# Rotating images by 90 degrees: the first 4 MB in neighbouring partitions, stored quadrant by quadrant

## Chip, cores and metric

The kernel runs on one core of a Trainium2 chip. The metric is the device time of one execution in microseconds (us), the median of several runs. Profiles come from one execution that the hardware profiler recorded.

## What is computed

The input is a batch of 32 x 3 images of 256 x 256 float32 values, 25.17 MB. Each image is turned by a quarter clockwise:

```
np.rot90(x, k=-1, axes=(-2, -1))
```

Output row j of an image is column j of the input, read from the bottom up. No arithmetic is done; 25.17 MB come in and 25.17 MB go out.

## The kernel before

All images are taken as one stack of 24576 rows of 256 values. R = 16 rows are one unit of 16 KB, so an image is 16 units. A group of size s holds 128 x s units: s units of 16 KB in each of 128 SBUF partitions. `sizes` is (2, 2, 2, 4, 2): five groups of 4.19, 4.19, 4.19, 8.39 and 4.19 MB, each with a tile of its own (u0 to u4), so that the whole input lies in SBUF and no buffer is used twice, apart from the small ones named below.

**Loads (lines 50 to 59).** A group is split into halves a = 0, 1 and into I = s interleaved sets i. One transfer fills the partitions i, i + I, i + 2I and so on, for both halves: 64 partitions x 2 rows of 16 KB for a group of size 2, and 32 partitions x 2 rows of 32 KB for the group of size 4, each 2 MB. The first and the last transfer are cut in two of 1 MB (lines 56 and 57), so there are 14 loads. All are issued by SP in the order of the program; the last but one is called `mark`.

**Turning (`turn_group`, lines 61 to 79).** VectorE's transpose turns blocks of 32 x 32 inside each block of 32 partitions (a quadrant). For a group of size 2 there are four such instructions, for the four quarters (low or high rows and columns of a unit), each 128 x 2048 elements; for the group of size 4 there are eight. They work in place. So the first quarter (line 69) is written to a spare tile in PSUM or to the tile `extra`, the other three (line 74) into the group's tile, and ScalarE then copies the first quarter to its place (line 79). The order in which elements are written, `c r k i`, is chosen so that after the transposes a partition holds whole output rows, of the images that its number stands for. VectorE takes the groups in order, and each waits for its loads.

**Stores (lines 81 to 87).** A group goes out by two transfers, even partitions and odd partitions: 64 partitions x s rows of 16 KB. The stores are issued by SP after all loads, and the first one waits for `mark`, so that loads and stores do not mix in the queue. Later stores stand behind it in the queue of SP. Each transfer uses one of eight semaphores in turn; a transfer that takes one again waits until its earlier user has landed.

Of the kernel before, what the change touches and what calls it, by code (L numbers as in the profile page):

```python
# [1 line left out]

# [4 lines left out]


@with_exitstack  # L10
def kernel(
    ctx: ExitStack,
    tc: tile.TileContext,
    x: bass.AP,
    out: bass.AP,
):

    nc = tc.nc
    fp32 = mybir.dt.float32

    B, C, H, W = x.shape
    P = nc.NUM_PARTITIONS
    R = 16
    E = R * W  # L30
    hw = R // 2
    low, high = slice(0, hw), slice(hw, R)

    rows_in = x.rearrange("b c h w -> (b c h) w")
    rows_out = out.rearrange("b c h w -> (b c h) w")

    sizes = (2, 2, 2, 4, 2)
    first = [sum(sizes[:n]) for n in range(len(sizes))]
    groups = [
        ctx.enter_context(tc.tile_pool(name=f"group{n}", bufs=1)).tile([P, s, E], fp32, name=f"u{n}")  # L40
        for n, s in enumerate(sizes)
    ]
    psum = ctx.enter_context(tc.tile_pool(name="psum", bufs=1, space=bass.MemoryType.PSUM))
    spare = [psum.tile([P, E // 2], fp32, name=f"spare{h}") for h in range(2)]
    extra = ctx.enter_context(tc.tile_pool(name="extra", bufs=1)).tile([P, E // 2], fp32, name="extra")

    def rows_of(rows, n):
        return rows[first[n] * P * R : (first[n] + sizes[n]) * P * R]

    for n in range(len(sizes)):  # L50
        I = sizes[n]
        ld = rows_of(rows_in, n).rearrange("(a i m r) w -> i m a (r w)", a=2, i=I, m=P // I)
        to = groups[n].rearrange("p s f -> p (s f)").rearrange("p (a f) -> p a f", a=2)
        for i in range(I):
            if (n, i) in ((0, 0), (len(sizes) - 1, I - 1)):
                mark = nc.sync.dma_start(out=to[i::I, 0], in_=ld[i][:, 0])  # L56
                nc.sync.dma_start(out=to[i::I, 1], in_=ld[i][:, 1])  # L57
            else:
                nc.sync.dma_start(out=to[i::I], in_=ld[i])

    def turn_group(n, held):
        I = sizes[n]
        T = I // 2
        K = W // (R * T)
        u = groups[n].rearrange("p s f -> p (s f)")
        src = u.rearrange("p (a t r g c) -> p t c r g a", a=2, t=T, r=R, c=R)
        dst = u.rearrange("p (i c k t r) -> p t c r k i", i=I, c=R, k=K, t=T)[:, ::-1, :, ::-1, ::-1, :]
        for t in range(T):
            nc.vector.transpose(  # L69
                out=held[t].rearrange("p (i c k r) -> p c r k i", i=I, c=hw, k=K)[:, :, ::-1, ::-1, :],  # L70
                in_=src[:, t, low, low])
        for c, r in ((low, high), (high, high), (high, low)):
            for t in range(T):
                nc.vector.transpose(out=dst[:, t, c, r], in_=src[:, t, c, r])  # L74
        back = u.rearrange("p (i c k t r) -> p t i c k r", i=I, c=R, k=K, t=T)[:, ::-1]
        for t in range(T):
            kept = held[t].rearrange("p (i c k r) -> p i c k r", i=I, c=hw, k=K)
            for i in range(I):
                nc.scalar.copy(out=back[:, t, i, low, :, high], in_=kept[:, i])  # L79

    for n, held in enumerate(([spare[0]], [extra], [spare[1]], spare, [extra])):
        turn_group(n, held)

    for n in range(len(sizes)):
        st = rows_of(rows_out, n).rearrange("(a i m r) w -> a m i (r w)", a=2, i=sizes[n], m=P // 2)
        for a in range(2):
            put = nc.sync.dma_start(out=st[a], in_=groups[n][a::2])
            if (n, a) == (0, 0):
                tc.add_manual_dep(put.ins, mark.ins.name, mybir.DependencyInfo(
                    mybir.DependencyClass.Sync, mybir.DependencyReason.SCHED_ONLY), reason="stores after loads")  # L90


# [1 line left out]
_INS = ['x']  # L94
_OUTS = [((32, 3, 256, 256), 'float32')]


# [23 lines left out]
```

## Time and profile before

| what | value |
|---|---|
| median of 3 runs | 123.49 us (123.46 to 123.56) |
| the profiled execution | 123.59 us |
| its span (first to last recorded event) | 121.8 us |
| VectorE busy | 86.9 us, 24 transposes |
| ScalarE busy | 13.2 us, 16 copies and a table load |
| moved by DMA | 50.33 MB, 413 GB/s over the span |
| issues on SP | 24 transfers: 14 loads, 10 stores |

Busy times are those of one engine's instructions added up. The slices cut the span in 40 equal parts, of 3.05 us each here; a digit is the busy share in tenths, and the line of GB/s is what the 16 DMA engines moved. "SPq" is SP's queue of transfers: its instruction issues a transfer and goes on, and the transfer lands later.

### The profile page before, as it was taken

How to read it: one execution, taken by the hardware profiler on the slowest of the kernel's cores; microseconds unless marked ns; L12 is line 12 of the kernel's file. 1: busy time of each engine (PE TensorE's matmuls, PEld its weight loads, DVE VectorE, ACT ScalarE, POOL GpSimd, SP SyncE). 2: the span in 40 equal slices, each digit the busy share in tenths (PEclk: the TensorE clock that was granted, in tenths of full speed). 3: DMA queues.
4: the chain of work that ended last, by engine and by line, in shares of the span. 5: the costliest groups of instructions: out<-in, count | busy, mean ns of one | idle time of the engine just before them, and what ended most of it. 6: DMA issues, size and time to landing. Idle time of an engine off the chain costs nothing.

```text
span 121.8 us, 131 instructions
## 1 busy us (share of the span) xinstructions
DVE 86.9 (71%) x24; ACT 13.2 (11%) x17; POOL 0.2 (0%) x4
## 2 busy tenths in 40 slices
DVE  0000599999999999999999999999999991000000
ACT  0000400006000060001400000003720006000000
POOL 0000000000000000000000000000000000000000
DMA  4999999999999999999999999999999999999994
GB/s 86 387 430 430 430 430 436 430 430 430 479 420 441 420 452 409 398 430 430 425 430 409 430 425 430 430 430 430 430 425 420 425 430 430 430 430 425 430 430 178
DMA packets 3200, 50.33 MB, mean 413 GB/s; under 512 B 384, under 2 KB 384, under 8 KB 384
## 3 DMA queue, kind: packets, MB, share of 16 engines
q1 hardware_dynamic: 3200, 50.33, 97.5%
HBM read 25.17 MB, written 25.17 MB: 413 GB/s over the span
## 4 chain that ended last, share of the span: by engine, by line
DVE 60%; issue 12%; DMA 9%; SPq 1%; ACT 1%; ACTq 1%; DVEq 0%
DVE u L74 42%; DVE spare L69 12%; DMA u<-in_x_dram 9%; DVE extra L69 6%; ACT u L79 1%; ACTq L116 1%; SPq L56 0%; SPq L57 0%; DVEq L69 0%
## 5 line engine op out<-in xcount | busy, mean ns | idle before, releaser
L74 DVE STREAM_TRANSPOSE u<-u 128x2048 f32<-128x2048 f32 x18 | 65.4, 3650 | 0.5
L69 DVE STREAM_TRANSPOSE spare<-u 128x2048 f32<-128x2048 f32 x4 | 14.2, 3581 | 13.5 <-DMA u<-in_x_dram 13.5
L79 ACT COPY u<-spare 128x512 f32<-128x512 f32 (+1 forms) x12 | 8.0, 743 | 51.7 <-DVE u L74 51.7
L69 DVE STREAM_TRANSPOSE extra<-u 128x2048 f32<-128x2048 f32 x2 | 7.7, 3862 | 0.0
L79 ACT COPY u<-extra 128x1024 f32<-128x1024 f32 x4 | 4.0, 1043 | 24.6 <-DVE u L74 24.6
L79 ACT ACT_TABLE_LOAD x1 | 1.3, 1283 | 13.5 <-DMA u<-in_x_dram 13.5
L105 POOL MEMSET const-bfloat16-1.0<- 128x1 bf16 x1 | 0.1, 101 | 0.0
L105 POOL MEMSET const-uint8-127<- 128x1 uint8 x1 | 0.1, 101 | 0.0
L105 POOL MEMSET const-float32-0.0<- 128x1 f32 x1 | 0.1, 98 | 0.2 <-issue 0.2
L105 POOL MEMSET const-float32-1.0<- 128x1 f32 x1 | 0.1, 98 | 0.0
## 6 DMA issues: line engine op xcount, KB each, us to landing
u<-in_x_dram SPq DMA_DIRECT2D x10, 2048.0 KB, 30.4
out_dram<-u SPq DMA_DIRECT2D x8, 2048.0 KB, 16.4
out_dram<-u SPq DMA_DIRECT2D x2, 4096.0 KB, 16.7
u<-in_x_dram SPq DMA_DIRECT2D x4, 1024.0 KB, 20.6
```

The lines of the kernel that those rows point to most:

```text
L69: nc.vector.transpose(out=held[t].rearrange("p (i c k r) -> p c r k i", i=I, c=hw, k=K)[:, :, ::-1, ::-1, :], in_=src[:, t, low, low])
L74: nc.vector.transpose(out=dst[:, t, c, r], in_=src[:, t, c, r])
L79: nc.scalar.copy(out=back[:, t, i, low, :, high], in_=kept[:, i])
L105: nc = _bacc.Bacc("TRN2", target_bir_lowering=False, num_devices=1)
L116: with _tile.TileContext(nc) as tc:
```

## The change

Group 0, the first 4.19 MB, is laid out differently; the other groups are not touched. It is loaded by two transfers, one per half a: unit p of the half goes to partition p, so neighbouring units lie in neighbouring partitions (128 partitions x one row of 16 KB, 2 MB each). Since an image is 16 units, a quadrant then holds two whole images of each half. In `turn_group` the elements of group 0 are written in the order `c r i k` in place of `c r k i`; the counts and sizes of the instructions are the same. The stores of group 0 go by quadrant q and half a: 16 partitions (every second one of 32) x 2 rows of 16 KB, 0.5 MB each, eight in place of two. The first load of the kernel is no longer cut in two, so there are 13 loads and 16 stores.

```diff
-    for n in range(len(sizes)):
+    ld = rows_of(rows_in, 0).rearrange("(a p r) w -> a p (r w)", a=2, p=P)
+    for a in range(2):
+        nc.sync.dma_start(out=groups[0][:, a], in_=ld[a])
+    for n in range(1, len(sizes)):
...
-            if (n, i) in ((0, 0), (len(sizes) - 1, I - 1)):
+            if (n, i) == (len(sizes) - 1, I - 1):
...
-        dst = u.rearrange("p (i c k t r) -> p t c r k i", i=I, c=R, k=K, t=T)[:, ::-1, :, ::-1, ::-1, :]
+        def to(tile, c, t):
+            if n == 0:
+                return tile.rearrange("p (i c k t r) -> p t c r i k", i=I, c=c, k=K, t=t)[:, ::-1, :, ::-1, :, ::-1]
+            return tile.rearrange("p (i c k t r) -> p t c r k i", i=I, c=c, k=K, t=t)[:, ::-1, :, ::-1, ::-1, :]
+        dst = to(u, R, T)
         for t in range(T):
-            nc.vector.transpose(
-                out=held[t].rearrange("p (i c k r) -> p c r k i", i=I, c=hw, k=K)[:, :, ::-1, ::-1, :],
-                in_=src[:, t, low, low])
+            nc.vector.transpose(out=to(held[t], hw, 1)[:, 0], in_=src[:, t, low, low])
...
-    for n in range(len(sizes)):
+    st = rows_of(rows_out, 0).rearrange("(a q i g r) w -> q a g i (r w)", a=2, q=4, i=2, r=R)
+    for q in range(4):
+        for a in range(2):
+            put = nc.sync.dma_start(out=st[q, a], in_=groups[0][q * P // 4 + a : (q + 1) * P // 4 : 2])
+            if (q, a) == (0, 0):
+                tc.add_manual_dep(put.ins, mark.ins.name, mybir.DependencyInfo(
+                    mybir.DependencyClass.Sync, mybir.DependencyReason.SCHED_ONLY), reason="stores after loads")
+    for n in range(1, len(sizes)):
         st = rows_of(rows_out, n).rearrange("(a i m r) w -> a m i (r w)", a=2, i=sizes[n], m=P // 2)
         for a in range(2):
-            put = nc.sync.dma_start(out=st[a], in_=groups[n][a::2])
...
+            nc.sync.dma_start(out=st[a], in_=groups[n][a::2])
```

More of the change, by code (lines that the diff above doesn't have):

```diff
@@ L82 @@
         turn_group(n, held)
-    for n in range(len(sizes)):
+    st = rows_of(rows_out, 0).rearrange("(a q i g r) w -> q a g i (r w)", a=2, q=4, i=2, r=R)
[6 more added lines that the diff above has]
+    for n in range(1, len(sizes)):
         st = rows_of(rows_out, n).rearrange("(a i m r) w -> a m i (r w)", a=2, i=sizes[n], m=P // 2)
         for a in range(2):
[L87 to L90, printed above, removed]
+            nc.sync.dma_start(out=st[a], in_=groups[n][a::2])
 _INS = ['x']
```

## The prediction, made before the changed kernel ran

> **What bounds the kernel now.** I read the busy shares and the slices of the page first, then the queue, then a table of windows cut where one group's transfers end and the next begin, then what SP waited for. On the page:
>
> ```profile
> DVE 86.9 (71%) x24; ACT 13.2 (11%) x17; POOL 0.2 (0%) x4
> ...
> DMA  4999999999999999999999999999999999999994
> GB/s 86 387 430 430 430 430 436 430 430 430 479 420 441 420 452 409 398 430 430 425 430 409 430 425 430 430 430 430 430 425 420 425 430 430 430 430 425 430 430 178
> ...
> q1 hardware_dynamic: 3200, 50.33, 97.5%
> ```
>
> The reader is to see that the 16 DMA engines are busy in every slice but the first and last, at 420 to 440 GB/s: 50.33 MB at 430 GB/s are 117.0 us of a span of 121.8. VectorE is busy for 71% only, ScalarE for 11%. The time is the time of the queue, as long as something always stands in it. The chain of waits names VectorE for 60%, because each transpose follows another without a gap; but the table of windows (columns: length, VectorE, ScalarE, GpSimd busy and count, TensorE clock, DMA share, GB/s) shows no fall of the rate:
>
> ```profile
> 2.00:13.40 11.40, 0.00 (x0) 0.00 (x0) 0.00 (x0) 1.00 1.01 402
> 13.40:33.00 19.60, 19.36 (x6) 3.21 (x3) 0.00 (x0) 1.00 1.02 435
> 33.00:52.40 19.40, 19.26 (x6) 1.99 (x2) 0.00 (x0) 1.00 1.00 429
> 52.40:62.20 9.80, 9.77 (x4) 1.93 (x2) 0.00 (x0) 1.00 1.01 430
> 62.20:71.90 9.70, 9.63 (x4) 0.00 (x0) 0.00 (x0) 1.00 0.99 421
> 71.90:91.50 19.60, 19.53 (x6) 4.11 (x8) 0.00 (x0) 1.00 1.01 427
> 91.50:111.20 19.70, 9.40 (x3) 1.99 (x2) 0.00 (x0) 1.00 1.01 429
> 111.20:121.80 10.60, 0.00 (x0) 0.00 (x0) 0.00 (x0) 1.00 0.84 357
> ```
>
> From 2.0 to 62.2 us the 25.17 MB come in, from 62.2 to 121.0 they go out. The rows are, in order: group 0 in; groups 1 and 2 in; group 3 in; group 4 in; group 0 out (4.19 MB in some 9.75 us); groups 1 and 2 out; group 3 out; group 4 out. Two rows matter below. Group 3 comes in by transfers that touch 32 partitions each, every fourth one, at 429 GB/s. Group 0 goes out by transfers that touch 64 partitions each, every second one, at 421 GB/s. Every transfer of the kernel before is spread over all 128 partitions in this manner. One more view, the DMA queue's own waits:
>
> ```profile
> SPq L87 <- DMA u<-in_x_dram: 31.1, 1, 31.1
> SPq L87 <- DVE u L74: 29.7, 2, 19.2
> ```
>
> The stores of group 0 are held only until the marked load has landed (31.1 us at one wait); groups 3 and 4 are held for VectorE (and briefly ScalarE), issued at 89.2 and 103.0 us, while the queue still has earlier stores: group 2 until 91.5, group 3 until 111.2. So VectorE has about 1 us of cover at group 3 (a first packet starts about 1.4 us after its issue: first issue at 0.73, first bytes at 2.1) and about 7 us at group 4.
>
> **The change, part by part.**
>
> *The loads of group 0.* Three transfers (1, 1 and 2 MB, 64 partitions) become two of 2 MB over 128 neighbouring partitions. Bytes and 16 KB rows are the same 256. One issue goes: L56 took 0.60 us and L57 0.57 us for 64 rows, L59 0.62 for 128; the first issue stays at about 0.6, so the first bytes still come at 2.1 us, and later issues lie beside running transfers. The stretch from 2.0 to 13.4 runs at 402 GB/s and not at 430; the missing 28/430 of 11.4 us are 0.74 us, and that bounds any gain: between 0 and -0.7 us. A loss is bounded by one issue, +0.6. I take 0: the slow part is the first packet of each engine, and the new load has such a packet too. Group 0's transposes need both transfers, that is all 4 MB, as before.
>
> *VectorE.* The four transposes of group 0 keep 2048 elements per partition; only the order of the written elements changes (inner run of 16 at a step of 64 B, outer 2, where it was inner 2 over 16). No row shows that order. The nearest rows: inner 2 takes 3.62 us, inner 4 (group 3) 3.55 to 3.70, the slowest of all (into the extra tile) 3.87. So I bound it by ±0.3 us each, ±1.2 us for four, take 0, and it is covered by 1 us at group 3 and by more if stores of group 0 take longer. Without cover the excess over 1 us, 0.2 us, would be seen. VectorE, ScalarE and their counts of instructions are otherwise unchanged.
>
> *Issue and waits of the stores.* Two stores become eight: six more issues on SP of at most 0.65 us (the first of L87 took 0.67, 128 rows; the new one has 32 rows), 3.9 us in all. They begin at 59.85 us while the last load still has 2.3 us to run; each carries 0.52 MB, 1.22 us of transfer at 430 GB/s, so SP is ahead of the queue by 1.22 - 0.65 us each time: nothing on the path. If issues took the 1.37 us that the slowest of group 0 to 2's stores took, eight would cost 11.0 us against 9.75 of transfer: +1.2 us, the upper bound. The built order shows new waits: the stores of group 1 now wait for the first and second store of group 0 to land, group 2 for the third and fourth, since eight semaphores are reused in turn. Behind them on SP stand only later stores, and six or more small stores are still queued when the first lands, so they cost 0. Group 3 and 4's stores are behind VectorE's waits as before.
>
> As the row first: the last 2 MB of loads are two queued transfers of 1 MB, and the window 52.4 to 62.2 holds 430 GB/s with them. [...]
>
> *What the stores read.* This is the part that decides. A store of quadrant q takes partitions 32q + a, 32q + a + 2, and so on: 16 partitions inside one block of 32. No row of before has that. Lower end: nothing, since 32 spread partitions (group 3's loads) still ran at 429 GB/s. Upper ends: the most that any row shows per partition is 429/32 = 13.4 GB/s; 16 partitions at that are 214 GB/s, and 4.19 MB take 19.6 us where 9.75 were: +9.85 us. By group 0's own old stores, 64 partitions at 430, it is 6.7 GB/s per partition, 107 GB/s, 39.2 us and +29.4; but group 3's row shows twice that per partition, so that end is unlikely. Between nothing and +9.85 I take +9.85: the row nearest in number of partitions is the one with 32, every row at full rate touches all four blocks of 32 and the new store touches one, and the smallest way in which 16 engines on a quarter of the partitions can collide, two on one path, gives the same factor of two. What follows the stores is only later stores of the same queue, so nothing hides it: the 9.85 us move the end in full.
>
> [...]
>
> **Sum.** Loads 0, VectorE 0, issues and waits 0, stores +9.85. The profiled execution took 123.59 us (span 121.8): 133.4. The median of the runs is 0.1 us below it, so I predict 133.3 us.
>
> **The rivals.**
>
> *Same (not slower).* The engines' own rate is the limit: each moves 430/16 = 26.9 GB/s, whichever partition it reads. For it: one rate in all rows, with 64 and with 32 partitions, in and out. Then the stores take 9.75 us as now: 123.5. It decides if one partition can give 26.9 GB/s, as 16 engines on 16 partitions would need; no row shows more than 13.4. A gain at the start by the 0.74 us above would make it faster, 122.8; against it, the first packets' delay stays.
>
> *Half of it.* Quadrants 0 and 1 stand ahead of 2 and 3 in the queue. If one engine of each colliding pair gets ahead by its whole share of the first two quadrants, the two halves of the partitions are read at once for half of the time, and the loss is 4.9 us: 128.4. Against it: all engines get their shares in the same order and start within a packet of each other (0.6 us).
>
> *VectorE or SP starves the queue at full store rate.* 0.2 us from VectorE and 1.2 us from slow issues: 124.9.
>
> *The stores go at a quarter.* 107 GB/s, +29.4: 152.9.
>
> **How the numbers follow.** Half rate 0.72 (133.3; with VectorE's ±1.2, now covered by 10 us of later stores, with the start's -0.7 to +0.6, and up to 2 us if the eight transfers add some gap of their own, 132 to 136). Half of the loss 0.09 (128.4). Same 0.11 (123.5). Faster 0.03 (122.8). Starved 0.02 (124.9). A quarter 0.03 (152.9). The range 128 to 136 holds the first two, 0.81, and leaves out the ends "nothing" and "a quarter", 0.19 together with their kin. About 0.2% is what a measurement of this kernel can tell from no change; faster by more 0.03, within 0.11, slower 0.86.
>
> **What would show it.** Half rate: in the slices after the loads' end, some six of 3.3 us each, 210 to 220 GB/s for some 19.6 us from 62 us on, with the DMA share still near 1 because packets last twice as long; 430 GB/s before and after; VectorE at 87 us as now; stores of group 3 no longer close to VectorE. If 62 to 72 us shows 420 to 430 GB/s, the step on the stores is wrong. If the rate there falls with a low DMA share, it is issue or waits, not the partitions. If the loads of group 0 end before 12.9 or after 13.9 us, the first step is wrong. The forecast fails if one block of 32 partitions can feed all 16 engines.

## The result and the profile after

The changed kernel takes 134.21 us (133.94 to 134.28, 5 runs) against 123.49 us (123.39 to 123.56, 5 runs): ratio 1.0865, 95% interval 1.0849 to 1.0881. That is 10.7 us slower; 133.3 us had been forecast. The profiled execution took 134.28 us, its span 132.5. From its page, busy shares, slices (3.31 us each) and queue:

```profile
DVE 87.1 (66%) x24; ACT 13.2 (10%) x17; POOL 0.2 (0%) x4
...
DMA  4999999999999999999798998999999999999993
GB/s 104 420 425 435 430 430 430 435 430 435 455 465 415 396 455 396 425 435 336 158 237 213 213 213 242 430 411 455 415 435 435 406 465 401 440 425 430 440 420 153
...
q1 hardware_dynamic: 3280, 50.33, 97.3%
```

The bytes are the same, and VectorE is busy as long as before. But in six slices in the middle the rate stands at 158 to 242 GB/s, 213 in three of them, while the DMA engines still count as busy (7 to 9 tenths). So the packets took longer (1.28 us each, as shown below), and the queue did not run empty. The table of windows of the changed kernel, with the same columns as before and the bounds between the groups moved to where they now lie:

```profile
2.00:13.70 11.70, 0.02 (x1) 1.28 (x1) 0.00 (x0) 1.00 0.97 396
13.70:62.40 48.70, 48.39 (x14) 5.85 (x6) 0.00 (x0) 1.00 1.00 425
62.40:72.20 9.80, 9.73 (x4) 0.00 (x0) 0.00 (x0) 1.00 1.01 214
72.20:82.90 10.70, 10.67 (x4) 0.08 (x1) 0.00 (x0) 1.00 0.99 227
82.90:92.70 9.80, 9.77 (x3) 4.03 (x8) 0.00 (x0) 1.00 1.01 431
```

The first two rows are the loads, the next two group 0's stores, the last is the start of group 1's. Only the stores of group 0 changed their rate: 214 GB/s where 421 stood. They take from 62.4 to about 82.9 us, 20.5 us for what had taken 9.7; the second of their rows shows 227 because its end already holds some of group 1's bytes. A closer look at 66 to 70 us, in 40 slices of 0.1 us, shows the packets themselves:

```profile
DMA  0000899700000000779900000000089990000000
GB/s 0 0 0 0 164 1639 656 164 0 0 0 0 0 0 0 0 164 164 1638 655 0 0 0 0 0 0 0 0 0 164 656 1311 492 0 0 0 0 0 0 0
DMA packets 80, 0.79 MB, mean 197 GB/s; under 512 B 32, under 2 KB 32, under 8 KB 32
q1 hardware_dynamic: 80, 0.79, 95.7%
```

A packet's bytes are booked where the packet starts, and each burst adds up to 16 of them (164 + 1639 + 656 + 164 GB/s over 0.1 us each are 0.26 MB), one for each of the 16 engines. Bursts are some 13 slices apart: all 16 engines start one 16 KB packet about every 1.3 us, in step. The last two lines give the time more exactly: 80 less the 32 small ones are 48 packets of 16 KB, and they took 95.7% of 16 engines' 4 us, so 1.28 us each, where 430 GB/s over 16 engines means 0.61 us. The kernel before has no gap longer than one slice at 66 to 70 us, and its 101 large packets took 0.62 us each:

```profile
GB/s 164 656 0 819 819 164 164 328 328 328 983 492 164 164 492 164 983 492 328 0 655 0 983 655 328 0 655 0 983 655 328 0 655 0 983 655 164 164 655 0
DMA packets 117, 1.65 MB, mean 414 GB/s; under 512 B 16, under 2 KB 16, under 8 KB 16
q1 hardware_dynamic: 117, 1.65, 97.7%
```

What SP's queue waited for, after:

```profile
SPq L96 <- DMA u<-in_x_dram: 31.1, 1, 31.1
SPq L103 <- DVE u L83: 12.0, 2, 9.6
```

The wait for the marked load is as long as before; that for VectorE fell from 29.7 to 12.0 us, since the later stores come later in the queue anyway.

### The profile page after: what moved, and what is told of

It is laid out like the page before. It is cut to its first block, busy times and chain, and to the rows that moved or that the text cites. A ratio compares the mean times of both kernels' runs of the same rounds, so it can differ in the third digit from the quotient of the medians.

```text
span 132.5 us, 135 instructions
## 1 busy us (share of the span) xinstructions
DVE 87.1 (66%) x24; ACT 13.2 (10%) x17; POOL 0.2 (0%) x4
## 3 DMA queue, kind: packets, MB, share of 16 engines
q1 hardware_dynamic: 3280, 50.33, 97.3%
## 4 chain that ended last, share of the span: by engine, by line
DMA 50%; DVE 14%; SPq 11%; ACT 1%; ACTq 1%; issue 1%
DMA u<-in_x_dram 43%; DVE u L83 11%; SPq L96 10%; DMA out_dram<-u 7%; DVE extra L80 3%; ACT u L88 1%; ACTq L129 1%; SPq L53 1%; SPq L63 1%
## 5 line engine op out<-in xcount | busy, mean ns | idle before, releaser
L80 DVE STREAM_TRANSPOSE spare<-u 128x2048 f32<-128x2048 f32 x4 | 14.2, 3583 | 13.7 <-DMA u<-in_x_dram 13.7
```

The source lines that it names most:

```text
L80: nc.vector.transpose(out=to(held[t], hw, 1)[:, 0], in_=src[:, t, low, low])
```

## Which part of the change, and what in it

**One part alone.** The first three kernels take the change apart. `stores_only` is the kernel before with only the store loop of the change:

```diff
+    for q in range(4):
+        for a in range(2):
+            put = nc.sync.dma_start(out=st[q, a], in_=groups[0][q * P // 4 + a : (q + 1) * P // 4 : 2])
```

> Before, with only group 0's stores changed to the eight of 16 partitions inside one block of 32; loads and the order of the transposes are those of before, so group 0's output rows land in other places. Theory (the partitions that a store reads set its rate): the whole 10.5 us that group 0's stores lose in the changed kernel (16 packets per engine at 1.27 us and not 0.61) are here too: 133.9 to 134.1 us. Rival (the new loads or transposes carry part of the loss): up to 0.9 us less, 133.3 us or below.

Measured: 134.38 us, ratio 1.0886 (1.0871 to 1.0900). The whole loss is in the stores. `wide_stores` is the opposite, the changed kernel with the old stores of group 0:

```diff
-            put = nc.sync.dma_start(out=st[q, a], in_=groups[0][q * P // 4 + a : (q + 1) * P // 4 : 2])
+        for put in [nc.sync.dma_start(out=st[a], in_=groups[0][a::2])]:
```

> The changed kernel, with group 0's stores back to two of 64 partitions, every second one; loads and transposes of group 0 are the changed ones, so its output rows land in other places. Theory: the loss goes; what is left is the 0.2 us by which the first group's loads ended later: 123.7 us. Rival (the loads and transposes cost what the prediction's sum lacked, 0.9 us): 124.4 us. Rival (the loads are a gain that the stores hide): 122.8 to 123.3 us.

Measured: 123.43 us beside 123.40 of before, ratio 1.0002 (0.9993 to 1.0011). The new loads and the new order of the transposes cost nothing and bring nothing; both rivals fall, and so do the 0.2 us that were expected of the start.

**The number of transfers.** `split8` keeps the old partitions and cuts the two stores in eight:

```diff
-            put = nc.sync.dma_start(out=st[a], in_=groups[n][a::2])
+                put = nc.sync.dma_start(out=st[a][:, i, cut], in_=groups[0][a::2, i, cut])
```

> Before, with group 0's two stores cut into eight of 0.5 MB that keep every second partition (64 partitions x 8 KB). Theory (partitions): no change, 123.5 us, 425 to 430 GB/s in group 0's stores. Rival (eight small transfers and their issues, of 1.8 to 2.6 us each in the changed kernel, set the rate): eight issues of 2.4 us, 133 us.

Measured: 123.55 us, ratio 1.0015 (1.0006 to 1.0024): 0.15 us for six more transfers, not 10. Its group 0 stores, the view of their line first and then the window 62.4 to 71.0:

```profile
L89 SPq DMA_DIRECT2D out_dram<-u x8: 511/1206/1329, 59.7 to 67.0; - x8
...
62.40:71.00 8.60, 8.57 (x3) 0.00 (x0) 0.00 (x0) 1.00 1.01 425
```

and the same line's view in the changed kernel (minimum, median and maximum of one issue in ns):

```profile
L96 SPq DMA_DIRECT2D out_dram<-u x8: 631/2368/2599, 60.1 to 73.3; - x8
```

The median issue takes 1.21 us here and 2.37 us there; 0.52 MB take 1.22 us at 430 GB/s and 2.45 us at 214. For these stores of 0.5 MB, an issue on the full queue lasted about as long as a transfer. So the long issues of the changed kernel are a consequence of slow transfers, though the chain of waits on its page puts 10% of the span on them (line 96):

```profile
DMA u<-in_x_dram 43%; DVE u L83 11%; SPq L96 10%; DMA out_dram<-u 7%; DVE extra L80 3%; ACT u L88 1%; ACTq L129 1%; SPq L53 1%; SPq L63 1%
```

`half64`, below, confirms it: it loses as much with two issues for group 0, which are done in 1.37 us:

```profile
59.76 1.37 SPq L95 DMA_DIRECT2D out_dram<-u  x2
```

**Which partitions.** Three kernels are the changed one with other sets of partitions per store of group 0:

```diff
-groups[0][q * P // 4 + a : (q + 1) * P // 4 : 2]
+groups[0][k::8]                       step8: 16 partitions, all blocks, eight stores
+groups[0][q * 32 : (q + 1) * 32]      block32: 32 neighbours, four stores
+groups[0][q * 64 : (q + 1) * 64]      half64: 64 neighbours, two stores
```

> The changed kernel, with group 0's eight stores over 16 partitions at a step of 8 (k, k+8, ... over all four blocks of 32) in place of 16 inside one block; group 0's output rows land in other places. Three theories differ. One block of 32 partitions has a rate of its own (214 GB/s): all four blocks serve, so full rate, 123.7 us. One partition gives at most 13.4 GB/s: still 16 partitions, 214 GB/s, 134 us. [...]

> The changed kernel, with group 0's stores as four of 32 neighbouring partitions (one whole block each, 1 MB); group 0's output rows land in other places. If one partition gives at most 13.4 GB/s, 32 give 429 GB/s: 123.7 us. If the position counts (one block, or shared paths): half rate as in the changed kernel, 134 us.

> The changed kernel, with group 0's stores as two of 64 neighbouring partitions (0 to 63, then 64 to 127, 2 MB each); group 0's output rows land in other places. If a block of 32 has a rate of its own of 214 GB/s, two blocks give 428: 123.7 us. If one partition gives at most 13.4 GB/s: full rate, 123.7 us. [...]

Measured: `step8` 133.68 us, ratio 1.0836 (1.0820 to 1.0853); `block32` 134.57 us, 1.0889 (1.0833 to 1.0946); `half64` 134.06 us, 1.0864 (1.0848 to 1.0881). In a window within their stores of group 0, for `step8`, `block32` and `half64` in turn (the last from 71.0 us on):

```profile
62.40:72.00 9.60, 9.53 (x4) 0.00 (x0) 0.00 (x0) 1.00 0.98 212
```

```profile
62.40:72.00 9.60, 9.56 (x3) 0.00 (x0) 0.00 (x0) 1.00 0.98 220
```

```profile
71.00:82.00 11.00, 10.93 (x4) 0.00 (x0) 0.00 (x0) 1.00 1.00 223
```

All three run at half rate. `half64` is the cleanest of them: it differs from `wide_stores` in nothing but the partitions, as its two transfers write the same rows of the output, in the same order and in the same pieces. So neither the addresses in DRAM nor the number or size of the transfers can be its cause. `wide_stores` in the same stretch (the start of group 1's stores lies in it):

```profile
71.00:82.00 11.00, 10.93 (x4) 0.00 (x0) 0.00 (x0) 1.00 1.01 429
```

32 partitions should have given 429 GB/s if each were worth 13.4, and 64 neighbours even more: the count of partitions falls as an explanation. 16 partitions over all four blocks should have been fast if a block of 32 had a rate of its own: that falls too. What is left is which partitions are taken together. Fast are 128 neighbours (the new loads, 396 GB/s with the start in their window), 64 at a step of 2 (429 GB/s in `wide_stores`) and 32 at a step of 4 (group 3's loads, 429), over the full width; slow are 64, 32 or 16 out of one half (223, 220 and 214), and 16 at a step of 8 (212). The windows of the slow sets show 212 to 223 GB/s, and the changed kernel's packets (1.28 us each) 205, about half of 430 in every case. Half the rate is what two engines that take turns on one path would give, as the prediction had it; but that is the author's reading, since no view shows the way from an engine to a partition. Why 16 at a step of 8 are slow where 32 at a step of 4 are fast is not shown either.

**The other direction.** `half_loads` is `wide_stores` with group 0 loaded in halves of the partitions:

```diff
-    ld = rows_of(rows_in, 0).rearrange("(a p r) w -> a p (r w)", a=2, p=P)
-    for a in range(2):
-        nc.sync.dma_start(out=groups[0][:, a], in_=ld[a])
+    ld = rows_of(rows_in, 0).rearrange("(a p r) w -> p a (r w)", a=2, p=P)
+    for h in range(2):
+        nc.sync.dma_start(out=groups[0][h * 64 : (h + 1) * 64], in_=ld[h * 64 : (h + 1) * 64])
```

> The changed kernel with the wide stores of group 0 (every second partition), and its loads as two over 64 neighbouring partitions (0 to 63, then 64 to 127, 2 MB each) in place of two over all 128; group 0's output rows land in other places. Theory (a set of neighbouring partitions reaches half of the paths, in both directions): group 0 lands some 9.8 to 10.5 us later, at about 23.5 us, and the end moves by as much, 133.5 to 134 us. Rival (only reads of SBUF collide, writes do not): 123.4 us.

Measured: 133.41 us, ratio 1.0811 (1.0792 to 1.0830). Its start:

```profile
2.10:21.70 19.60, 0.00 (x0) 0.00 (x0) 0.00 (x0) 1.00 1.02 214
```

The same 214 GB/s when SBUF is written. For 64 neighbours the rate is halved in both directions (223 GB/s in `half64`, 214 here); the other slow sets were not tried with loads.

## Can the loss be taken back

**The order of the quadrants.** The author supposed that two engines collide only while they are at the same half of the partitions; then changing the half more often lets one that has a lead use it. `order02` takes the quadrants as 0, 2, 1, 3, `alternate` changes after every transfer:

```diff
+    for q, a in ((0, 0), (2, 0), (0, 1), (2, 1), (1, 0), (3, 0), (1, 1), (3, 1)):
```

> The changed kernel, with the quadrants stored in the order 0, 2, 1, 3. Theory (pairs of engines read the same path in step): two quadrants of different halves now follow each other after 2 packets x 2, but engines stay in step, so little is won: 132 to 134 us. Rival (the queue lets an engine run ahead, so two quadrants of different halves are read at once): up to half of the loss or more comes back, 124 to 129 us.

> The changed kernel, with the eight stores in an order that changes the half of the partitions after every transfer: quadrants 0, 2, 0, 2, 1, 3, 1, 3. The order 0, 2, 1, 3 (three changes of half) gave 132.9 us, 1.3 us below the changed kernel's own order (one change). Theory (engines of a pair in step collide; each change of half gives back twice the lead of one over the other, some 0.3 us at first): seven changes, 128 to 132 us, growing as the lead grows. Rival (the order does not matter and 1.3 us were of another kind): 133 to 134 us.

Measured: `order02` 132.90 us, ratio 1.0764 (1.0738 to 1.0789); `alternate` 129.09 us, 1.0458 (1.0442 to 1.0475). The second is the changed kernel with eight lines in another order, and gives back 5.1 of its 10.7 us. Its window and its slices from 66 to 70 us:

```profile
62.40:71.00 8.60, 8.57 (x3) 0.00 (x0) 0.00 (x0) 1.00 1.05 312
...
GB/s 819 328 0 164 0 164 164 164 492 1147 164 0 492 164 328 1147 328 164 328 0 164 0 164 0 0 328 328 655 164 328 328 492 655 492 328 328 164 328 655 164
DMA packets 113, 1.26 MB, mean 315 GB/s; under 512 B 36, under 2 KB 36, under 8 KB 36
q1 hardware_dynamic: 113, 1.26, 94.2%
```

The gaps between the bursts are gone: the engines are no longer in step, and the rate is 312 GB/s. The 77 large packets took 0.78 us each, between the 0.62 of the kernel before and the 1.28 of the changed one. To be out of step is not enough, though. In `half64` at 66 to 70 us there are no such gaps either, and its 49 packets took 1.29 us each:

```profile
GB/s 164 328 983 164 0 164 164 164 0 164 0 328 0 164 819 492 164 0 328 0 164 0 164 164 164 0 164 1147 164 164 164 164 164 0 164 0 164 164 164 0
DMA packets 49, 0.80 MB, mean 201 GB/s; under 512 B 0, under 2 KB 0, under 8 KB 0
q1 hardware_dynamic: 49, 0.80, 98.5%
```

There each transfer keeps the engines in one half for eight packets (128 rows over 16 engines), so a lead of a packet or two leaves them all in the same half. In `alternate` the half changes after two packets (32 rows over 16 engines), so the same lead puts an engine into the other half. That the gain grows with the number of changes, from 1.3 to 5.1 us, agrees with this; it remains the author's estimate, as which engine collided with which is not recorded. `alternate` is not a version that beats the kernel before.

**Another queue.** `two_queues` issues quadrants 2 and 3 from ScalarE, `pool_queue` all eight stores from GpSimd (the edit shown):

```diff
-            put = nc.sync.dma_start(out=st[q, a], in_=groups[0][q * P // 4 + a : (q + 1) * P // 4 : 2])
+            put = nc.gpsimd.dma_start(out=st[q, a], in_=groups[0][q * P // 4 + a : (q + 1) * P // 4 : 2])
```

> The changed kernel, with quadrants 2 and 3 stored from ScalarE's queue, where they come after some copies of group 3, at about 85 us, beside stores of other groups from SP's queue. Theory (an engine held by another on its path does nothing else): if the other queue's packets put the engines out of step, the second half of the loss shrinks, 129 us; quadrants 0 and 1 alone still lose 5.2 us. Rival (the loss is per packet, wherever it stands): 134 us.

> The changed kernel, with group 0's eight stores issued from GpSimd's queue, which does nothing else, at the same point (after the marked load), beside the other groups' stores on SP's queue. Nothing empties the queues here, unlike with ScalarE's queue. Theory (two engines collide only while both are at a store of a quadrant): the other queue's packets put them out of step and part of the loss goes, 125 to 131 us. Rival (a colliding packet holds its engine and the two stay in step): 134 us.

`two_queues` took 152.19 us, ratio 1.2330 (1.2312 to 1.2348), which neither side had expected, and it tells nothing on the question. Its windows:

```profile
62.40:72.00 9.60, 9.53 (x4) 0.00 (x0) 0.00 (x0) 1.00 0.93 191
72.00:87.60 15.60, 15.57 (x5) 2.25 (x5) 0.00 (x0) 1.00 0.00 0
```

and its SP queue's waits:

```profile
SPq L103 <- DMA out_dram<-u: 25.2, 1, 25.2
```

For 15.6 us no byte moved. Group 1's first store on SP waited 25.2 us for a store of group 0: it takes the semaphore that a store of ScalarE's had in turn, and that one stood behind copies that waited for VectorE (ScalarE issued its first store at 86.5 us). `pool_queue` has no such hole and took 135.60 us, ratio 1.0985 (1.0968 to 1.1002). Its page's slices:

```profile
GB/s 113 431 426 436 426 436 431 436 426 494 401 411 460 460 411 382 426 436 392 303 264 318 269 303 299 303 299 289 289 357 445 416 445 416 445 416 436 426 406 59
```

The two queues share the engines at about 300 GB/s from 63 to 99 us, and the loss is 12.2 us, a little more than in one queue. The rival's 134 us is nearer. The lines of its queues (q1 is SP's, q0 GpSimd's) show where the time went:

```profile
q1 hardware_dynamic: 2896, 46.14, 83.3%
q0 software_dynamic: 384, 4.19, 13.6%
```

Group 0's 256 large packets took 13.6% of 16 engines' 133.9 us, 1.14 us each in place of 1.28, which is some 2 us less per engine. But the other 46.14 MB took some 3 us per engine more than in the changed kernel (83.3% of 133.9 us, where 97.3% of 132.5 us less 16 packets of 1.28 us are left there). So group 0's packets did become a little shorter beside the others, as the theory had it, and the others became longer by more than that. Why they did is open.

**The start.** `first32` is the kernel before with group 0 loaded by eight transfers of 32 partitions, every fourth:

```diff
+                        nc.sync.dma_start(out=to[i + 2 * v :: 4, a], in_=quarter[a, i, v])
```

> Before, with group 0 loaded by eight transfers of 32 partitions (every fourth, 0.5 MB each) in place of three. The start (0.74 us missing at 402 GB/s) would gain if the last engine's first packet came earlier with two rows per engine in the first transfer: 123.0 to 123.2 us. Rival (the first packets' delay does not depend on it, or eight issues of 0.6 us delay the later ones): 123.4 to 123.7 us.

Measured: 124.59 us, ratio 1.0094 (1.0078 to 1.0110). Slower, and by more than the rival had said. Group 0's first transpose waited 14.5 us and not 13.5; the windows 5 to 8 and 8 to 11 us have 399 and 393 GB/s, where the kernel before has 404 and 431:

```profile
5.00:8.00 3.00, 0.00 (x0) 0.00 (x0) 0.00 (x0) 1.00 1.03 399
8.00:11.00 3.00, 0.00 (x0) 0.00 (x0) 0.00 (x0) 1.00 0.96 393
```

The DMA share is near 1 in both, so packets took longer and the queue did not run empty. Why they did is open.

## Why the prediction was right, point by point

**The bound** was read rightly: the DMA queue sets the end, and the loss in one stage, 20.5 us for what had taken 9.7, moved the end in full, by 10.7 us. One reading was too tidy: between the first and the last slice the page shows 387 to 479 GB/s, not 420 to 440; the windows, which carry the argument, show 402 to 435 up to the last.

**The stores** were the step that decided, at +9.85 us. The window 62.4 to 72.2 us shows the 214 GB/s of the forecast, but it counts bytes where packets start; by the time of the packets themselves the rate was 205 GB/s. The forecast's 214 is a packet of twice 0.61 us, 1.22, and 1.28 was measured. Each engine moves 16 packets of group 0 (4.19 MB over 16 engines), and 16 times 0.06 us are the 0.9 us that the sum lacked.

Of the three reasons given for the term, two fall. The price came from a most of 13.4 GB/s per partition. That was an average over 32 partitions, of which the 16 engines were at about 16 at a time: the time of the packets adds up to 97.5% of the 16 engines' span, so by the author's estimate each engine has one under way. A large packet is one row of one partition (3200 packets less 384 small ones are 2816, as many as the kernel's 2560 rows of 16 KB and 256 of 32 KB), so 0.62 us per packet already means 26.5 GB/s from a single partition in the kernel before, and 0.78 us means 21 GB/s in `alternate`, whose stores have 16 partitions each. That no row showed more than 13.4 was therefore a misreading, and `block32` and `half64`, with two and four times the partitions, ran no faster. The second reason, that the new store touches one block of 32 and not four, falls with `step8`. The third, two engines on one path, is left: the half rate of every slow set (205 to 223 GB/s) and the 5.1 us that the order of the quadrants gave back agree with it, though no run shows a path. That 16 times 13.4 comes to the same 214 GB/s as two engines on one path is luck.

**The loads** were taken at 0 between -0.7 and +0.6 us: `wide_stores`, 1.0002, agrees. One detail was wrong: an issue over 128 neighbouring partitions took 0.39 to 0.42 us, not 0.6, and some bytes moved before 2.0 us; but the rate up to 13.7 us was 396 GB/s where the old loads had 402 up to 13.4, so nothing came of it.

**VectorE** was taken at 0 within ±1.2 us: three of group 0's four transposes went from 3.62 to 3.70 us on average, 0.2 us in all, and the later stores cover it (SP's wait for VectorE fell from 29.7 to 12.0 us).

**Issues and waits** were taken at 0 with 1.2 us as the upper bound: `split8` shows 0.15 us for six more transfers. The up to 2 us for a gap of the eight transfers' own, which the range allowed for, is shown by no run; those 0.15 us were measured in its place. The issue's duration, forecast at 0.65 us, was 2.37, but as shown above that follows from the transfers.

**The rivals.** "Same" fell because the engines did not get their 26.9 GB/s from every set of partitions (16.4 KB in 1.28 us are 12.8), though one partition gave 26.5 in the kernel before; "half of it" did not come in the order as built, and `alternate` comes close to its price (129.09 us against 128.4): half of the loss, 5.1 of 10.7 us, came back once the halves of the partitions were mixed in the queue. That the halves don't collide with each other was an assumption of that rival, which no run had shown by then. "Starved" fell with `split8` (0.15 us) and with the DMA share of 1.01 in the slow stretch, and "a quarter" with the rate of 214 GB/s.

## What to carry to other kernels

Choose the partitions of a transfer so that it is spread over the whole width at a small step (64 partitions at a step of 2 and 32 at a step of 4 ran at about 430 GB/s here, and loads over all 128 neighbours cost nothing against the old ones: 123.43 beside 123.40 us). Stores from 64 or 32 neighbours, from 16 in one block of 32, or from 16 at a step of 8 ran at half of it (windows of 212 to 223 GB/s), and so did loads into 64 neighbours (214 GB/s); more transfers in the same queue didn't make up for it (134.21 us with eight, 134.06 with the two of `half64`). The sign of it here was a rate that halved (from 421 to 214 GB/s) while the DMA share stayed at 1.01; where the rate fell together with the share (both 0 for 15.6 us in `two_queues`), it was a wait. Where a layout forces such sets, let neighbours in the queue come from different halves: that alone gave 5.1 of 10.7 us back.

## What the runs showed of the hardware beyond that

An issue on SP grew longer once several transfers were queued: the first two stores of the changed kernel were issued in 0.70 and 0.63 us, the other six in 1.81 to 2.60. For stores of 0.5 MB the median was 1.21 us at full rate and 2.37 us at half rate, about the time of one transfer (1.22 and 2.45 us). For larger stores it was shorter than the transfer: in the kernel before, an issue of L87 took at most 1.40 us, where 2 MB take 4.9 us at 430 GB/s. Issue time on a full queue was no cost of its own here (`split8`, 0.15 us for six more issues). Stores issued from GpSimd beside SP's stores were no way around the loss (135.60 us against 134.21). Cutting the first 4 MB into eight loads of 32 partitions cost 1.2 us, where cutting the stores of the same group in eight cost 0.15.
